# Forget logits from the value columns' sweep, key bias as rows for VectorE, reordered units of the mixer

## The chip, the core and the metric

The kernel runs on one core of a Trainium2 chip. The core has a matrix engine (TensorE, PE in the profile, with its weight loads as PEld), VectorE (DVE), ScalarE (ACT), GpSimd (POOL) and SyncE (SP), whose queue issues every DMA here. Each engine works through its own list in order and waits on semaphores for the others. SBUF is the memory on the core (128 partitions), PSUM takes the products of TensorE, DRAM is the memory outside. The metric is the device time of one launch in microseconds; lower is better.

## The reference

Two transformer blocks over 256 tokens of width 1024, in float32. The change lies in the mixer of the first block, whose input projection gives the queries, keys and values of a forgetting attention, its forget logits (eight columns), and four inputs of a gated recurrence:

```python
SPLITS = (FOX_WIDTH, FOX_WIDTH, FOX_WIDTH, FOX_HEADS, HGRN_WIDTH, HGRN_WIDTH, HGRN_WIDTH, HGRN_WIDTH)
hn = rmsnorm(h, norm_mix_g[l])
proj = hn @ w_in[l]
fq, fk, fv, ff, gq, gf, gi, gg = jnp.split(proj, split_idx, axis=-1)
log_f = jax.nn.log_sigmoid((ff + fox_f_bias[l]).astype(jnp.float32)).transpose(0, 2, 1)
fox_out = fox_attention(to_heads(fq), to_heads(fk), to_heads(fv), log_f)
...
F = jnp.cumsum(log_f, axis=-1)
s = jnp.einsum('bhqd,bhkd->bhqk', qi, k).astype(jnp.float32) * scale
s = s + Fi[..., None] - F[:, :, None, :]
s = jnp.where(mask, s, -jnp.inf)
p = jax.nn.softmax(s, axis=-1)
```

There are eight heads of width 64. The term of the query, F at t, is the same for a whole row of the softmax and falls out; the term of the key, minus F at s, is the key bias of the text.

## The kernel before

Every float32 product with a weight is made of three passes with operands split into a rounded high part and the rest: xh and xl for the activations, wh and wl for the weights. The weights stream in granules of 2048 values per partition (1 MB). SP loads a granule into one of three raw buffers, ScalarE casts half of it to wh (line 141), VectorE subtracts to get wl (line 142); six such halves, called parts, can stand ready.

The work is a list of units, one weight part each, with short pieces attached to them. A unit of a_units keeps weight blocks stationary and moves 256 token columns: 24 products. A unit of b_units keeps token blocks stationary and moves 512 weight columns: 12 products, six for token half t=0 and then six for t=1; four such units make 512 output columns and their sums are taken out of PSUM after the fourth. TensorE follows the list exactly as written. The other engines and SP get their order from a planner that works with the listed order as priority, so an operation of theirs can stand well before or after the place where it is listed.

The mixer has 36 units. Counted from 0: f (0 to 3) and q (4 to 7) of the recurrence, its gate (8 to 11), queries of the attention (12 to 15), its keys (16 to 19), its values (20 to 23), the recurrence's input gi (24 to 27), and keys of the memory for the cross attention (28 to 35). The pieces between them:

- The recurrence runs as nine levels, levels[0] to levels[8]: products on TensorE (lines 824, 804, 802, 853), then two decays (lines 813, 814) and a predicated copy on VectorE. The products of a level need the decays of the level before. They follow units 10, 11 and 13 to 19.
- forget() follows unit 12. It multiplies the eight logit columns of w_in, loaded on their own as wf (line 724) and split into wfh and wfl (lines 714, 715), in 24 products into one PSUM tile; then log-sigmoid and a cumulative sum on VectorE and ScalarE give minus F as high rows 0 to 7 and low rows 32 to 39 of the SBUF tile nF.
- For each of four pairs of heads there are three pieces: S (fox_scores, causal_exp), T (transposes of the probabilities) and V (products with the values). In S, two q k products of K = 64 per token tile are followed by two bias products (line 929): a selector column of sel, broadcast, times nF. The diagonal mask is added by VectorE in the pass that also finds the row's minimum (line 357); ScalarE takes the exponential; GpSimd and VectorE normalise each one half (line 938), one unit later. S of pairs 0 to 3 follows units 20, 21, 23 and 28; T 22, 25, 29 and 32; V 24, 27, 31 and 34.
- The memory rows are loaded after unit 12, normalised, and transposed after units 25 and 26 through PSUM tiles of the pool s, which has four buffers in turn. The differential attention's lambda is worked out by VectorE (line 737 and on) from small loads.

PSUM pools: mm and tp have two buffers each, s has four. The differential attention in block 2 has a piece of the same form as S, without bias products (line 1176).

## Time and profile before

| | |
|---|---|
| median of 3 runs | 922.87 us (921.74 to 923.49) |
| span of the profiled execution, first to last instruction | 918.8 us |
| TensorE busy | 904.6 us, 98% of the span |
| VectorE busy | 589.3 us, 64% |
| ScalarE busy | 489.4 us, 53% |
| GpSimd busy | 125.5 us, 14% |
| DMA | 160.79 MB, mean 175 GB/s |

The profiled execution's own time outside the span is not recorded; the 4.1 us between span and median stand for it. Times in the rows are microseconds from the span's start. Products are pipelined and their ends are modelled: what a product costs in a row of products is the step from its start to the next one's, not its duration. A bracket at the end of a timeline row says how long the engine was idle before it and which operation ended that.

### The profile page before, as it was taken

The page shows a single profiled execution, that of the slowest core. Times are in us where ns is not written, and L with a number is a line of the kernel's source. Part 1 is how long each engine was busy: PE and PEld are TensorE (multiplying, and loading weights), DVE is VectorE, ACT ScalarE, POOL GpSimd, SP SyncE. Part 2 cuts the span into 40 slices and gives each one's busy share as a digit, 9 for nine tenths or more (in the row PEclk, how much of TensorE's full clock was granted, in tenths as well). Part 3 has the DMA queues.
Part 4 walks back from the last instruction along what each step waited for, and adds up shares of the span by engine and source line. Part 5 has one row for each costly group of instructions (what it writes and reads, how often), then busy time and mean ns, then how long its engine had stood idle before and what let it go on. Part 6 is the DMA issues. An engine that isn't in the chain of part 4 may idle for free.

```text
span 918.8 us, 15164 instructions
## 1 busy us (share of the span) xinstructions
PE 904.6 (98%) x6203; PEld 823.5 (90%) x6203; DVE 589.3 (64%) x861; ACT 489.4 (53%) x741; POOL 125.5 (14%) x134
## 2 busy tenths in 40 slices
PE   8999999999999999999999999999999999999996
PEld 7889799899899999999899899999998789999995
DVE  5787666764675554445686555776656777766664
ACT  6763644555455444444564454657443676555552
POOL 3200110000002111111104000221301201101101
PEclk9999999999999999999999999999999999999998
DMA  8774344544465555565374555334655455555531
GB/s 260 253 245 141 130 153 169 197 148 138 161 204 184 185 184 183 184 186 188 134 271 139 184 181 187 128 115 140 216 178 190 159 185 182 186 199 192 167 131 46
DMA packets 116819, 160.79 MB, mean 175 GB/s; under 512 B 4551, under 2 KB 89357, under 8 KB 116749
## 3 DMA queue, kind: packets, MB, share of 16 engines
q1 hardware_dynamic: 116749, 159.82, 52.2%
q8 instruction: 48, 0.79, 0.3%
q14 instruction: 22, 0.18, 0.1%
HBM read 158.76 MB, written 1.05 MB: 174 GB/s over the span
## 4 chain that ended last, share of the span: by engine, by line
PE 89%; DVE 3%; DMA 2%; ACT 2%; issue 1%; POOL 1%; SPq 1%; DVEq 0%; POOLq 0%; ACTq 0%
PE mm L205 19%; PE mm L206 19%; PE mm L207 19%; PE s L206 8%; PE s L207 8%; PE s L205 8%; DMA w<-in_w_in_dram 2%; DVE wl L142 1%; PE s L804 1%; PE tp L336 1%; POOL sm L296 1%; PE tp L1032 1%; PE s L1024 1%; ACT wh L141 1%; DMA lamv<-in_lambda_k_dram 1%
## 5 line engine op out<-in xcount | busy, mean ns | idle before, releaser
L142 DVE TENSOR_TENSOR wl<-w,wh 128x1024 fp32r<-128x1024 f32 x283 | 354.0, 1257 | 191.8 <-ACT wh L141 190.1
L141 ACT CAST wh<-w 128x1024 fp32r<-128x1024 f32 x284 | 296.8, 1051 | 305.6 <-PE mm L206 199.2
L205 PE MATMUL mm<-xh,wh 128*128 128x256 f32 x1120 | 317.5, 283 | 0.4 <-ACT r L765 0.4
L206 PE MATMUL mm<-xl,wh 128*128 128x256 f32 x1120 | 313.1, 280 | 0.3
L207 PE MATMUL mm<-xh,wl 128*128 128x256 f32 x1120 | 312.5, 279 | 0.0
L205 PEld LDWEIGHTS mm<-xh,wh 128*128 128x128 f32 x1120 | 210.6, 188 | 4.3 <-issue 2.0
L206 PEld LDWEIGHTS mm<-xl,wh 128*128 128x128 f32 x1120 | 210.6, 188 | 2.1 <-DVE xl L328 0.7
L207 PEld LDWEIGHTS mm<-xh,wl 128*128 128x128 f32 x1120 | 210.5, 188 | 0.0
L205 PE MATMUL s<-wh,mh 128*128 128x512 f32 x176 | 70.1, 398 | 0.0
L206 PE MATMUL s<-wl,mh 128*128 128x512 f32 x176 | 69.6, 395 | 0.0
L207 PE MATMUL s<-wh,ml 128*128 128x512 f32 x168 | 66.4, 395 | 0.0
L296 POOL TENSOR_TENSOR sm<-sm,half 128x1 f32<-128x1 f32 (+2 forms) x24 | 20.2, 842 | 214.9 <-DVE sm L309 203.9
L1067 POOL TENSOR_TENSOR r<-r 128x512 f32<-128x512 f32 x16 | 25.4, 1584 | 149.1 <-ACT r L1065 149.1
L205 PE MATMUL mm<-eh,wh 128*128 128x256 f32 x160 | 45.6, 285 | 0.0
L206 PE MATMUL mm<-el,wh 128*128 128x256 f32 x160 | 44.7, 279 | 0.0
L207 PE MATMUL mm<-eh,wl 128*128 128x256 f32 x160 | 44.6, 279 | 0.0
L207 PE MATMUL s<-wh,mh 128*128 128x512 f32 x112 | 44.3, 396 | 0.0
L1326 POOL TENSOR_TENSOR r<-r 128x512 f32<-128x512 f32 x11 | 21.4, 1946 | 148.6 <-DVE r L1314 124.8
L206 PE MATMUL s<-wl,ml 128*128 128x512 f32 x104 | 41.1, 396 | 0.0
L205 PE MATMUL s<-wh,ml 128*128 128x512 f32 x104 | 41.1, 395 | 0.0
L205 PE MATMUL mm<-wh,xh 128*128 128x512 f32 x96 | 39.4, 410 | 0.5 <-ACT xh L324 0.4
L206 PEld LDWEIGHTS s<-wl,mh 128*128 128x128 f32 x176 | 33.1, 188 | 7.2
(272 smaller groups left out, 1365.3 us busy)
## 6 DMA issues: line engine op xcount, KB each, us to landing
w<-in_w_in_dram SPq DMA_DIRECT2D x41, 1024.0 KB, 5.3
w<-in_w_dram SPq DMA_DIRECT2D x32, 1024.0 KB, 4.8
w<-in_w_up_dram SPq DMA_DIRECT2D x22, 1024.0 KB, 5.0
w<-in_w_down_dram SPq DMA_DIRECT2D x11, 1024.0 KB, 5.1
w<-in_w_xkv_dram SPq DMA_DIRECT2D x8, 1024.0 KB
w<-in_w_out_dram SPq DMA_DIRECT2D x8, 1024.0 KB, 6.1
w<-in_w_xq_dram SPq DMA_DIRECT2D x4, 1024.0 KB, 4.7
w<-in_w_xo_dram SPq DMA_DIRECT2D x4, 1024.0 KB, 5.8
```

What stands on the lines that cost most here:

```text
L141: S.copy(hi, src)
L142: low.tensor_tensor(lo, src, hi.bitcast(F32), op=ALU.subtract)
L205: PE.matmul(o, lh, rh, start=first, stop=False)
L206: PE.matmul(o, lh, rl, start=False, stop=False)
L207: PE.matmul(o, ll, rh, start=False, stop=last)
L296: G.tensor_tensor(r[:, :n], v[:, :n], half.to_broadcast([P, n]), op=ALU.pow)
L336: PE.transpose(o[:, k * P:(k + 1) * P], xn[:, kk * P:(kk + 1) * P], ident)
L804: PE.matmul(o, k_[:, x], q2, start=True, stop=True)
L1024: PE.matmul(s[:, t, :], xq[:, j, t * P:(t + 1) * P], xkT[:, j, :], start=(c == 0), stop=(c == 1))
L1032: PE.matmul(o[:, c * T:(c + 1) * T], xv[:, m, cs], pt[:, m, :], start=(m == 0), stop=(m == 1))
L1067: G.tensor_tensor(tt, ra, ra, op=ALU.mult)
L1326: G.tensor_tensor(yv, yg, yv, op=ALU.mult)
```

## The change

The separate load, split and products of the eight logit columns go. The value columns are swept with 520 columns, values and logits together: fv_units makes two products of 260 columns where there was one of 512, in two mm and two tp tiles, and takes the logits out as two tiles of 128 tokens by eight, which forget() turns with two transposes. Minus F goes to a DRAM tile, negF, and comes back as rows on all partitions (load_bias, two DMAs a pair); GpSimd adds the diagonal mask to it; VectorE adds the result where it added the mask, so the bias products, nF and sel go. The values now stand in units 12 to 15, queries and keys alternate in 16 to 23. The levels follow units 9, 11, 12, 13, 14 and 16 to 19, forget() follows 15. S follows units 21, 23, 26 and 28; T 23, 27, 30 and 32; V 25, 29, 32 and 34. Comments are removed; nothing behind the mixer is touched.

```diff
     def causal_exp(s, bias):
...
-                V.tensor_tensor_reduce(pm[:, e, TILES[i]], s[e][:, TILES[i]], bias[:, (1 - i) * P:T], -1.0, 3e38,
+                V.tensor_tensor_reduce(pm[:, e, TILES[i]], s[e][:, TILES[i]], bias(e, i), -1.0, 3e38,
...
         def tables():
...
-            V.tensor_copy(r32(wfh), wf)
-            V.tensor_tensor(r32(wfl), wf, wfh, op=ALU.subtract)
-            V.tensor_tensor(r32(sel), ident[:, 0:8], ident[:, 32:40], op=ALU.add)
-            G.memset(nF, 0.0)
...
         def load_tables():
...
-                nc.sync.dma_start(wf.rearrange("p (k c) -> p k c", k=8),
-                                  w_in[:, 1536:1544].rearrange("(k p) c -> p k c", p=P))
...
+    def fv_units():
+        gs_ = [Granule(w_in[kq * 512:(kq + 1) * 512, 1024:1544], 4, 520, False) for kq in range(2)]
+        st = {}
+        def unit(i):
+            if i == 0:
+                st["o"] = [(mm_t(), tp_t()) for _ in range(2)]
+            w = part(gs_[i // 2], i % 2)
+            for t in range(2):
+                tok = slice(t * P, (t + 1) * P)
+                for k in range(2):
+                    for c in range(2):
+                        cs = slice(c * 260, (c + 1) * 260)
+                        mm3(st["o"][t][c][:, 0:260], r32(xh[:, 2 * i + k, tok]), r32(xl[:, 2 * i + k, tok]),
+                            w[0][:, k, cs], w[1][:, k, cs], i == 0 and k == 0, i == 3 and k == 1)
+            release()
+            def ev():
+                for t in range(2):
+                    copy = V.tensor_copy if t else S.copy
+                    o = st["o"][t]
+                    ff.append(sm_t())
+                    copy(fv[:, t, 0:260], o[0][:, 0:260])
+                    copy(ff[t], o[1][:, 252:260])
+                    copy(fv[:, t, 260:512], o[1][:, 0:252])
+            return ev if i == 3 else None
...
+    fox_bias = [x.rearrange("p (e c) -> p e c", e=2) for x in
+                (R[3][:, 1024:1792], R[0][:, 512:1280], R[0][:, 1280:2048], R[1][:, 0:768])]
     def forget():
-        o = tp_t()[0:8, 0:T]
-        wh, wl = (r32(x).rearrange("p (k c) -> p k c", k=8) for x in (wfh, wfl))
-        for k in range(8):
-            mm3(o, wh[:, k, :], wl[:, k, :], r32(xh[:, k, :]), r32(xl[:, k, :]), k == 0, k == 7)
-        z = R[3][0:8, 0:768].rearrange("p (i t) -> p i t", i=3)
+        o = s_t()[0:8, 0:T]
+        for t in range(2):
+            PE.transpose(o[:, t * P:(t + 1) * P], ff[t], ident)
+        z = p_t()[0:8, :].rearrange("p (i t) -> p i t", i=3)
...
-            V.tensor_copy(r32(nF[0:8, :]), z[:, 2, :])
-            V.tensor_tensor(r32(nF[32:40, :]), z[:, 2, :], nF[0:8, :], op=ALU.subtract)
-        then(cum)
+        then(cum, lambda: nc.sync.dma_start(negF, z[:, 2, :]))
+    def load_bias(*pairs):
+        def go():
+            for p in pairs:
+                row = negF[2 * p:2 * p + 2, :].rearrange("(o e) t -> o e t", o=1)
+                nc.sync.dma_start(fox_bias[p][:, :, 0:P], row[:, :, 0:P].to_broadcast([P, 2, P]))
+                nc.sync.dma_start(fox_bias[p][:, :, P:3 * P], row.to_broadcast([P, 2, T]))
+            def mask():
+                for p in pairs:
+                    for e in range(2):
+                        b = fox_bias[p][:, e, :].rearrange("p (n s) -> p n s", n=3)[:, 0:3:2, :]
+                        G.tensor_tensor(b, b, causal[:, P:T].unsqueeze(1).to_broadcast([P, 2, P]), op=ALU.add)
+            then(lambda: None, mask)
+        return go
     def fox_scores(p):
...
-                          start=True, stop=False)
-            for e in range(2):
-                hd = 2 * p + e
-                sh = r32(sel[:, hd:hd + 1]).to_broadcast([P, P])
-                PE.matmul(s[e][:, tile], sh, r32(nF[:, 0:(t + 1) * P]), start=False, stop=True)
-        pm, sums = causal_exp(s, causal)
+                          start=True, stop=True)
+        pm, sums = causal_exp(s, lambda e, i: fox_bias[p][:, e, TILES[i]])
...
+    u_ += fv_units()
+    for g in range(2):
+        u_ += a_units(cols(w_in, 0, g), XT, ev_to(R[2][:, g * 512:(g + 1) * 512], 0.125))
+        u_ += a_units(cols(w_in, 512, g), XT, ev_to(R[2][:, 1024 + g * 512:1024 + (g + 1) * 512]))
+    u_ += rows(w_in, 2568, 1, gi) + grid(xkw, 0, 4, R[5], None, ME)
     fox = Heads(fox_scores, fox_turn, fox_pv)
...
+    run(u_, {
+        1: [lambda: start.vectors()], 2: [lambda: start.load_tables()], 6: [lambda: start.tables()],
+        7: [lambda: start.load_later()], 9: [levels[0]], 11: [levels[1]],
+        12: [m_load, levels[2], lambda: start.difference()], 13: [levels[3]], 14: [levels[4]], 15: [forget],
+        16: [levels[5], m_s0], 17: [levels[6]], 18: [levels[7], m_s1, load_bias(0)], 19: [levels[8]],
+        20: [load_bias(1, 2, 3)], 21: [fox.S(0)], 23: [fox.T(0), fox.S(1)], 25: [fox.V(0), m_t0],
+        26: [fox.S(2), m_t1], 27: [fox.T(1)], 28: [fox.S(3), h_out(0)], 29: [fox.V(1), h_out(1)],
+        30: [fox.T(2)], 31: [h_turn(0)], 32: [fox.V(2), fox.T(3)], 33: [h_turn(1)], 34: [fox.V(3)],
+    })
```

## Rows read from the trace of the kernel before

**Rows 1.** Page part 1: busy time of each engine, share of the span, instructions; weight loads of part 5

```profile
PE 904.6 (98%) x6203; PEld 823.5 (90%) x6203; DVE 589.3 (64%) x861; ACT 489.4 (53%) x741; POOL 125.5 (14%) x134
L205 PEld LDWEIGHTS mm<-xh,wh 128*128 128x128 f32 x1120 | 210.6, 188 | 4.3 <-issue 2.0
```

**Rows 2.** Waits of TensorE, 20 to 220 us: who waited for whom, total us, times, longest

```profile
PE s L804 <- DVE r L825: 0.8, 1, 0.8
```

**Rows 3.** Windows table, 44.5 to 72 us: busy us and instructions of each engine, clock, DMA

```profile
44.50:72.00 27.50, 26.70 (x220) 25.19 (x219) 24.03 (x35) 16.61 (x25) 1.11 (x2) 1.00 0.74 253
```

**Rows 4.** Timeline of TensorE, 54 to 61 us: start, duration, line, operation, count

```profile
54.72 0.28 PE L205 MATMUL tp<-xh,wfh 128*8 128x256 f32 x1
...
57.45 0.28 PE L205 MATMUL mm<-xh,wh 128*128 128x256 f32 x1
...
60.25 1.89 PE L804 MATMUL s<-r,r 128*128 128x64 f32 x16
```

**Rows 5.** Timeline of TensorE, 90 to 101 us: first score piece and first transposes

```profile
91.04 0.49 PE L924 MATMUL s<-r 64*128 64x128 f32 x4
...
92.80 0.40 PE L205 MATMUL mm<-wh,xh 128*128 128x512 f32 x1
...
100.25 0.82 PE L345 MATMUL tp<-ident,P 128*128 128x128 f32 x6
```

**Rows 6.** Timeline of TensorE, 570 us: a score piece of block 2

```profile
570.06 0.93 PE L1176 MATMUL s<-r,r 64*128 64x128 f32 x8
570.91 0.38 PE L205 MATMUL mm<-xh,wh 128*128 128x256 f32 x1
```

**Rows 7.** Chain of waits, 90 to 101 us: start, us from step to step, operation

```profile
91.53 0.37 PE s L929 x2
...
99.95 0.23 PE mm L206
...
100.41 0.66 PE tp L345 x6
```

**Rows 8.** Timeline of TensorE at three unit ends: the first operation behind each

```profile
50.03 0.44 PE L804 MATMUL s<-r,r 128*128 128x64 f32 x2 [0.80 <-DVE r L825]
...
69.43 0.44 PE L804 MATMUL s<-r,r 128*128 128x64 f32 x3
...
78.60 0.44 PE L804 MATMUL s<-r,r 128*128 128x64 f32 x3
```

**Rows 9.** Timeline of VectorE near the same places

```profile
41.89 0.29 DVE L737 TENSOR_TENSOR lamv<-lamv 128x128 f32<-128x128 f32 x1 [3.65 <-DMA lamv<-in_lambda_k_dram]
...
70.04 2.34 DVE L142 TENSOR_TENSOR wl<-w,wh 128x1024 fp32r<-128x1024 f32 x2
...
78.80 0.69 DVE L269 COPY r<-mm 128x512 f32<-128x512 f32 x1 [0.57 <-PE mm L207]
```

**Rows 10.** Groups of VectorE, 0 to 160 us: busy us, mean ns, idle before

```profile
L325 DVE TENSOR_TENSOR ml<-tp,mh 128x256 fp32r<-128x256 f32 x4 | 1.7, 416 | 0.0
```

**Rows 11.** Timeline of VectorE: the forget scan and the first score operation

```profile
66.92 0.67 DVE L913 TENSOR_TENSOR_SCAN r<-r 8x256 f32<-8x256 f32 x1
...
93.36 0.28 DVE L357 CUSTOM_DVE_ANT_0 P<-s,causal 128x128 f32<-128x128 f32 x1
```

**Rows 12.** Timeline of GpSimd: two operations of one form, and the normalisation of pair 0

```profile
27.89 2.78 POOL L773 TENSOR_SCALAR r<-r 128x512 f32<-128x512 f32 x1 [11.77 <-DVE r L771]
...
31.45 1.06 POOL L773 TENSOR_SCALAR r<-r 128x512 f32<-128x512 f32 x1
...
95.93 0.84 POOL L938 TENSOR_SCALAR P<-P,sm 128x128 f32<-128x128 f32 x2 [35.81 <-DVE sm L934]
```

**Rows 13.** DMA issues of the whole span: queue, count, KB each, median us to landing

```profile
out_dram<-h SPq DMA_DIRECT2D x8, 128.0 KB, 1.8
...
g<-in_norm_mix_pre_dram SPq DMA_DIRECT2D x1, 512.0 KB, 6.9
```

**Rows 14.** Waits of the queue on SP, 0 to 240 us: total, times, longest

```profile
SPq L122 <- DVE wl L142: 130.1, 23, 9.0
```

More of the change, by code (lines that the diff above doesn't have):

```diff
@@ L60, in two_blocks @@
     small = ctx.enter_context(tc.tile_pool(name="small", bufs=16))
+    dram = ctx.enter_context(tc.tile_pool(name="dram", bufs=1, space=bass.MemoryType.DRAM))
     psum = ctx.enter_context(tc.tile_pool(name="psum", bufs=2, space=bass.MemoryType.PSUM))
@@ L611, in two_blocks @@
     lvl = const.tile([P, 512], U8, name="lvl")
-    sel = const.tile([P, 8], F32, name="sel")
-    nF = const.tile([P, T], F32, name="nF")
     vt = const.tile([P, 190], F32, name="vt")
@@ L620, in two_blocks @@
     pw = const.tile([P, 4, P], F32, name="pw")
-    wfh = const.tile([P, 64], F32, name="wfh")
-    wfl = const.tile([P, 64], F32, name="wfl")
+    negF = dram.tile([8, T], F32, name="negF")
     nlam = lam[:, 2:3]
@@ L683, in start @@
         lvlf = ppool.tile([P, 768], F32, tag="PT", name="lvlf")
-        wf = ppool.tile([P, 768], F32, tag="PT", name="wf")[:, 0:64]
         pieces = []
@@ L722, in load_tables @@
             nc.sync.dma_start(lvlf[:, 0:512], a["c_lvl"])
-            with nc.allow_non_contiguous_dma("eight columns"):
-                nc.sync.dma_start(wf.rearrange("p (k c) -> p k c", k=8),
-                                  w_in[:, 1536:1544].rearrange("(k p) c -> p k c", p=P))
             nc.sync.dma_start(fbias, a["fox_f_bias"].rearrange("o h -> h o"))
@@ L893, in h_turn @@
         return go
-    def forget():
-        o = tp_t()[0:8, 0:T]
-        wh, wl = (r32(x).rearrange("p (k c) -> p k c", k=8) for x in (wfh, wfl))
-        for k in range(8):
-            mm3(o, wh[:, k, :], wl[:, k, :], r32(xh[:, k, :]), r32(xl[:, k, :]), k == 0, k == 7)
-        z = R[3][0:8, 0:768].rearrange("p (i t) -> p i t", i=3)
+    ff = []
+    def fv_units():
[22 more added lines that the diff above has]
+            return ev if i == 3 else None
+        return [(lambda i=i: unit(i), gs_[i // 2] if i % 2 == 0 else None) for i in range(4)]
+    fox_bias = [x.rearrange("p (e c) -> p e c", e=2) for x in
+                (R[3][:, 1024:1792], R[0][:, 512:1280], R[0][:, 1280:2048], R[1][:, 0:768])]
+    def forget():
+        o = s_t()[0:8, 0:T]
+        for t in range(2):
+            PE.transpose(o[:, t * P:(t + 1) * P], ff[t], ident)
+        z = p_t()[0:8, :].rearrange("p (i t) -> p i t", i=3)
         V.tensor_scalar(z[:, 0, :], o, fbias, None, op0=ALU.add)
@@ L1177, in d_scores @@
                           start=True, stop=True)
-        pm, sums = causal_exp(s, bias)
+        pm, sums = causal_exp(s, lambda e, i: bias[:, (1 - i) * P:T])
         def norm():
```

10 lines of the change are left out of this document (removed).

## The prediction, made before the result was known

> **What bounds the kernel now.** I read the page first: TensorE is busy for 98% of the span, every other engine for 64% or less [rows 1]. Then the waits of TensorE in the mixer, which is the only stretch that the diff touches: from 20 to 220 us the list has two entries, and the larger is 0.8 us at the first level product behind VectorE's line 825 [rows 2]. So from 20 us on the kernel is a queue of products with no gap worth naming. Whatever leaves that queue leaves the time, and whatever makes TensorE wait adds to it. Last, the engine that could start to set the pace: in the stretch with the recurrence levels VectorE is busy 24.03 of 27.5 us, 87% [rows 3]. The weight loads are no bound: their queue entry mostly waits for VectorE to free a buffer [rows 14].
>
> **Removed: the forget products.** In the trace 24 products with an 8-column weight run from 54.72 to 57.45, when the next unit begins [rows 4]: 2.73 us of pure queue. Nothing else filled that time on TensorE. Minus 2.73 us.
>
> **Removed: the key bias products.** One score piece of the forgetting attention lasts from 91.04 to 92.80, 1.76 us [rows 5]; the other three pieces have the same pattern. Without the four bias products it is the piece that the differential attention of block 2 already has, same shapes and same K of 64: 570.06 to 570.91, 0.85 us [rows 6]. Four times 0.91 is 3.64 us. A lower bound is the smaller of a piece's two bias groups in the chain of waits, 0.37 us [rows 7], for each of the eight groups: 3.0 us. I take 3.64, since the block 2 piece is the same code without the bias.
>
> **Added: eight columns in the value sweep.** Four units go from 12 products of 512 columns (0.23 us each in the chain [rows 7], 2.8 us a unit) to 24 products of 260. The nearest unit has 24 products of 256 columns and takes 57.45 to 60.25, 2.80 us [rows 4]; times 260/256 is 2.84. Plus 0.04 a unit, with rounding plus 0.2 us for four. The price on the other side is the weight loads: 48 more, 188 ns each by the page [rows 1], 9.0 us if none were hidden. The 256-column unit has twice the loads of the 512-column one and the same length, so they are hidden, and I take 0.2.
>
> The Trainium skill speaks against this edit: TensorE: Matmul & The Clock Gate, Part 3 (The mechanism), says that a weight load overlaps products in flight only when their row groups differ, and all of these use every row. With the figure of the same page for a load (columns over 1.2, so 107 ns for 128 columns) 48 loads in the open would be an estimated 5.1 us, and the sum below would end at 922.2. The trace disagrees, by the two units of equal length.
>
> **Added: two transposes and their wait.** Six transposes take 0.66 us in the chain [rows 7], so two cost 0.2. The wait is new in kind: the transposes stand directly behind the last value product in TensorE's fixed order, and their input is the evicted 8-column piece. Half t=0 is complete half a unit earlier and ScalarE can take it out meanwhile; half t=1 goes through VectorE as a 260-column copy and then the 8-column one. An idle VectorE begins such a copy 0.2 us after the unit's end (78.60 and 78.80 [rows 8, 9]); 256 columns from PSUM take 0.42 us [rows 10], the small one less. So 0.4 (only the small copy is left) to 0.9 us if VectorE is idle. If it is behind, as at the unit end of 69.43, its splits run to 72.38 [rows 8, 9]: 2.9 plus 0.6, 3.5 us. The change leaves that unit's end without a level of its own, but the level before it is still being finished there. I take 1.0, near the idle end, and keep 0.4 to 3.5. Behind the waiting transposes stand all later products; nobody else waits for them soon.
>
> **Moved: the diagonal level goes from unit 10 to unit 9.** The 0.8 us wait at 50.03 is for VectorE's product of q and f [rows 2, 8]; one more unit (2.8 us) lies between the two now. Minus 0.8, with 0 as the other bound: VectorE had stood in line 737 until the lambda loads landed, at 41.89 [rows 9], and that wait may stay where it is. What is late next is the split of weights, which has buffers ahead.
>
> **Moved: the forget logits' way to the scores.** Before, the logits were a sum in SBUF 10.1 us after the last forget product (57.45, scan from 66.92 for 0.67 [rows 4, 11]). Now they also go to DRAM, come back as rows on all partitions, and GpSimd adds the mask. Write: 1.8 us, the landing time of the output rows; read: up to 6.9 us, the slowest broadcast of 512 KB (ours is 384 KB a pair) [rows 13]. Mask: two operations of 256 columns. The nearest GpSimd operation, 512 columns, took 1.06 us in one place and 2.78 beside VectorE's splits [rows 12], so half of that, 0.53 to 1.39 each. In sum, from the end of unit 15: 1.2 (wait and transposes), 10.1, 1.8, 6.9 and 1.1 to 2.8 is 21.1 to 22.8 us. The scores' VectorE operations of unit 21 need it after six units of 2.8, two level pieces of 1.9 (the row at 60.25 [rows 4]), leaving out two smaller ones, the 1.2, and 1.4 from the piece's start (2.3 before, 91.04 to 93.36 [rows 5, 11], less 0.9): 23.2. It fits by 0.4 us or more, so nothing on TensorE; if the cover is gone, each further microsecond arrives at the transposes of pair 0 after another 1.6 us. That spare: before, they began 9.2 us after the score piece (100.25 [rows 5]) and the normalisation ended 5.7 after it (95.93 plus 0.84 [rows 12]); now they come after 0.85 and two units, 6.45, against 4.8.
>
> The Trainium skill, SBUF — State Buffer (Who interferes with whom), says that a VectorE operation with two SBUF inputs and a GpSimd operation that reads SBUF shut each other out for a whole instruction. The 2.78 against 1.06 us agrees; by that rule the masks belong at the long end, which leaves the sum as it is and feeds the rivals below.
>
> **Other edits, at nothing.** The load of eight-column pieces, the two splits of it, the selector and one memset go from a stretch in which TensorE does not wait for them. Four more evictions of VectorE and ScalarE lie beside products. On SP's queue one write and eight loads stand among the weight loads; a weight load that comes late has the split buffers as cover, and the waits of that queue, up to 9.0 us [rows 14], cost TensorE nothing now. The second transpose of the memory rows has its PSUM tiles freed only one unit before, 0 to 1 us; I take 0.
>
> **Sum.** Minus 2.73, minus 3.64, plus 0.2, plus 0.2, plus 1.0, minus 0.8: minus 5.8 us. The span of the profiled execution is 918.8, the median of the three runs 922.87, so 4.1 us lie around the span and don't change. 922.87 less 5.8 is 917.1. With every unknown at its good end (wait 0.4, and another 0.4 us of the first waits gone) it is 916.1; with every one at its bad end (wait 3.5, the 0.8 kept, bias products at 3.0, 1 us at the memory rows) 922.0.
>
> **Rivals.**
> First, VectorE sets the pace between the levels: the 2.73 us of forget products were time in which it caught up, and it is 87% busy. Then the new wait is 3.5 instead of 1.0: 919.6. For it: the queue at 69.43. Against: at 78.60 it was idle at the same place.
> Second, the bias comes 1 to 4 us later than it may at the transposes of pair 0, through a slow load or masks: 918 to 921, middle 920. For it: the 0.4 us of cover. Against: each term of that chain was taken at its slow end.
> Third, slower. GpSimd works in order, and six masks of pairs 1 to 3 are listed ahead of the normalisation of pair 0. They wait for loads that may start only after unit 19, and if these stand behind a weight load for the 9.0 us seen on that queue, they land 15.9 us after unit 19; two masks after the last landing and the 0.84 make 19.5. The transposes are due after 12.1 (two units, 0.85, two units). TensorE then stands 7.4 us or, with all six masks after the landing, 12.9. The kernel is slower than before by more than can be taken for noise from a stall of 7.7 on; the middle is about 927. For it: the order of the list. Against: six masks before the scores' exponentials are done need no luck if the loads come soon.
> Fourth, the 48 extra weight loads come into the open: up to 9.0 us at 188 ns each, half of that 4.5, so 921.6 and no gain. For it: the load's length against the 0.12 us of a 260-column product. Against: the two units of equal length.
>
> **How the numbers follow.** My sum 0.62 (917.1, own range 915.5 to 919), the first rival 0.17 (919.6), the second 0.11 (920), the third 0.05 (927), the fourth 0.05 (921.6). A measurement of this kernel tells about 0.2%, 1.85 us, from no change: faster is below 921.0. Faster: 0.62, 0.17 and most of 0.11, so 0.86. Same: 0.05 and the rest, 0.08. Slower: 0.06. The range of 8 in 10 goes from 915.0 to 921.2; above it lie the third and the fourth case and a part of the second, below 916.1 only stalls that the trace does not show me.
>
> **What would show it.** The score piece lasts 0.85 us and no products with 8 columns are left. A value unit lasts 2.8 to 2.9; at 3.1 or more the weight loads came out. TensorE has one new entry in its waits, the forget transposes behind VectorE's copy, 0.4 to 3.5 us. The wait at the first level is gone. The transposes of pair 0 wait for nothing; if they do, GpSimd or a load is behind it and I am in the second or third case. The forecast is wrong if TensorE's idle time in the mixer grows by more than 3 us.

## The result and the profile after

The changed kernel takes 913.71 us (median of 4 runs, 913.16 to 916.50), the kernel before on the same chip 923.18 us (4 runs): ratio 0.9904, 95% interval 0.9887 to 0.9922. It is faster, by 9.5 us and not by the 5.8 of the forecast, and 913.71 lies below the range of 915.0 to 921.2. So the direction was right, and the size was wrong.

Four views of the changed kernel, in the order in which I read them. First, part 1 of the page: busy time of each engine, share of the span, instructions. TensorE has 6.6 us less to do than in [rows 1] and is as full as it was.

```profile
PE 898.0 (98%) x6213; PEld 823.9 (90%) x6213; DVE 588.4 (64%) x858; ACT 488.8 (54%) x743; POOL 130.0 (14%) x141
```

Second, the waits of TensorE from 20 to 220 us, the stretch of [rows 2] (who waited for whom: total us, times, longest). The wait at the first level is gone. The new entry at line 924 was foreseen, the larger one at line 346 was not.

```profile
PE tp L346 <- ACT PT L983: 0.6, 1, 0.6
PE s L924 <- DVE sm L910: 0.5, 1, 0.5
```

Third, the timeline of TensorE at the places of [rows 4, 5, 8] (start, duration, line, operation, count; the level pieces are clipped by the window asked for): the end of the gate sweep; a value unit; the forget transposes; the first score piece; the first transposes of probabilities; T(3); the start of the output stage.

```profile
48.46 0.78 PE L792 MATMUL s<-r,r 128*128 128x64 f32 x6
...
50.16 0.36 PE L206 MATMUL mm<-wh,xh 128*128 128x260 f32 x1
...
53.13 1.11 PE L792 MATMUL s<-r,r 128*128 128x64 f32 x9
...
67.14 0.27 PE L924 MATMUL s<-ident,sm 128*8 128x128 f32 x1
67.90 0.27 PE L924 MATMUL s<-ident,sm 128*8 128x128 f32 x1 [0.49 <-DVE sm L910]
67.93 0.37 PE L206 MATMUL mm<-xh,wh 128*128 128x256 f32 x1
...
90.79 0.93 PE L961 MATMUL s<-r 64*128 64x128 f32 x8
91.65 0.39 PE L206 MATMUL mm<-xh,wh 128*128 128x256 f32 x1
...
97.46 0.82 PE L346 MATMUL tp<-ident,P 128*128 128x128 f32 x6
...
136.05 0.55 PE L346 MATMUL tp<-ident,P 128*128 128x128 f32 x3
137.17 0.55 PE L346 MATMUL tp<-ident,P 128*128 128x128 f32 x3 [0.57 <-ACT PT L983]
137.47 0.36 PE L206 MATMUL mm<-eh,wh 128*128 128x256 f32 x1
...
147.81 0.40 PE L206 MATMUL s<-wh,mh 128*128 128x512 f32 x1
```

The score piece lasts from 90.79 to 91.65, 0.86 us. The value unit lasts 2.97. To see where the two profiled executions part, here are four lines: the first product of the gate sweep and of the output stage in before, then the first product of the gate sweep and the last product of all in the changed kernel.

```profile
35.70 0.39 PE L205 MATMUL mm<-wh,xh 128*128 128x512 f32 x1
...
153.39 0.39 PE L205 MATMUL s<-wh,mh 128*128 128x512 f32 x1
```

```profile
35.19 0.40 PE L206 MATMUL mm<-wh,xh 128*128 128x512 f32 x1
...
905.28 0.40 PE L208 MATMUL s<-wh,ml 128*128 128x512 f32 x1
```

The output stage begins 5.58 us earlier. Of these, 0.51 lie ahead of the gate sweep and 5.07 between it and the output stage, where all terms of the sum have their place; 5.8 were foretold. The surplus lies elsewhere.

Fourth, GpSimd's timeline, for the way of the logits: masks of pair 0, masks of the other pairs, normalisation of pair 0.

```profile
84.02 3.16 POOL L951 TENSOR_TENSOR r<-r,causal 128x256 f32<-128x256 f32 x2 [8.16 <-DMA r<-negF]
90.62 2.57 POOL L951 TENSOR_TENSOR r<-r,causal 128x256 f32<-128x256 f32 x4 [3.45 <-DMA r<-negF]
93.63 1.81 POOL L951 TENSOR_TENSOR r<-r,causal 128x256 f32<-128x256 f32 x2 [0.44 <-issue]
95.82 0.90 POOL L971 TENSOR_SCALAR P<-P,sm 128x128 f32<-128x128 f32 x2 [0.38 <-DVE sm L967]
```

One correction to the forecast's ground stands in the runs themselves: the changed kernel's profiled execution took 914.16 us with a span of 912.3, and every other profiled execution also has 1.8 us around its span. So the profiled execution of before, span 918.8, took about 920.6 and not 922.87: it was an execution 2.3 us better than the median, and the waits in it were small ones. The shortest of the 108 executions of this kernel timed in later comparisons took 920.72, so the profile shows the best case.

### The profile page after: what moved, and what is told of

The parts are those of the page before. It is cut to its first block, busy times and chain, and to the rows that moved or that the text cites. A ratio compares the mean times of both kernels' runs of the same rounds, so it can differ in the third digit from the quotient of the medians.

```text
span 912.3 us, 15217 instructions
## 1 busy us (share of the span) xinstructions
PE 898.0 (98%) x6213; PEld 823.9 (90%) x6213; DVE 588.4 (64%) x858; ACT 488.8 (54%) x743; POOL 130.0 (14%) x141
## 4 chain that ended last, share of the span: by engine, by line
PE 90%; DVE 4%; ACT 2%; DMA 2%; POOL 1%; issue 1%; SPq 0%; DVEq 0%; POOLq 0%; ACTq 0%
PE mm L206 19%; PE mm L207 19%; PE mm L208 19%; PE s L208 8%; PE s L206 8%; PE s L207 8%; DMA w<-in_w_in_dram 2%; PE s L792 1%; POOL sm L297 1%; DVE wl L143 1%; PE tp L1068 1%; PE s L1060 1%; PE tp L337 1%; ACT wh L142 1%; PE s L1212 1%
## 5 line engine op out<-in xcount | busy, mean ns | idle before, releaser
L143 DVE TENSOR_TENSOR wl<-w,wh 128x1024 fp32r<-128x1024 f32 (+1 forms) x283 | 355.4, 1261 | 182.4 <-ACT wh L142 180.8
L142 ACT CAST wh<-w 128x1024 fp32r<-128x1024 f32 (+1 forms) x284 | 296.1, 1048 | 306.0 <-PE mm L207 190.2
L206 PEld LDWEIGHTS s<-wh,mh 128*128 128x128 f32 x176 | 33.1, 188 | 6.7
```

The lines of the kernel that those rows point to most:

```text
L142: S.copy(hi, src)
L143: low.tensor_tensor(lo, src, hi.bitcast(F32), op=ALU.subtract)
L206: PE.matmul(o, lh, rh, start=first, stop=False)
```

## The experiments

**Both kernels again, and the diagonal level alone.** `b_again` is the kernel before and `a_again` the changed kernel, without any edit. `b_lev9` and `a_lev10` exchange the place of the diagonal level:

```diff
 b_lev9 (from before)
-             7: [lambda: start.load_later()], 10: [levels[0]], 11: [levels[1]]})
+             7: [lambda: start.load_later()], 9: [levels[0]], 11: [levels[1]]})
 a_lev10 (from the changed kernel)
-        7: [lambda: start.load_later()], 9: [levels[0]], 11: [levels[1]],
+        7: [lambda: start.load_later()], 10: [levels[0]], 11: [levels[1]],
```

> The kernel before once more, unchanged, timed against itself. It tells whether the profiled execution (span 918.8 us, so about 920.6 with the 1.8 us that lie around the span of every execution of the kernel after) is typical of the timed ones (921.7 to 923.9). Theory A, a cliff at the start: in most executions the wait at the first level product (0.8 us in the profile) is longer, because the lambda loads that VectorE stands waiting for land later; then the new profile shows more than 0.8 there, up to 3.5, and its span grows by the same. Theory B, the pace of the products: the span differs by some tenths of a per cent through all stages alike, with the same waits. Ratio 1.000 in both.

> The kernel before with one part of the change alone: the diagonal level follows unit 9 instead of 10. Theory A: the wait at the first level product goes whole, 3 to 4 us in the timed runs, ratio about 0.996. Theory B: only the 0.8 to 1.0 us of the profile go, ratio 0.999.

> The kernel after with that part undone: the diagonal level follows unit 10 again, everything else as in the change. Theory A: 3 to 4 us of the 9.5 come back, about 917, ratio to the kernel before 0.994. Theory B: 0.8 to 1.0 come back, ratio 0.991 to 0.992.

> The kernel after once more, unchanged, on the same chip as the three others. The first comparison gave a ratio of 0.9904 (0.9887 to 0.9922), my sum 0.9937. Theory A: 0.990 again. Theory B, chance differences of pace between single executions: nearer to my sum, 0.992 to 0.994.

Measured: b_again 923.43 (ratio to before 0.9983 to 1.0016), b_lev9 920.77 (0.9969 to 0.9991), a_lev10 914.57 (0.9889 to 0.9928), a_again 915.45 (0.9891 to 0.9931). The earlier level is worth 0.8 to 2.9 us in before and nothing in the changed kernel, whose waits have no entry at the first level in either place. So neither theory holds whole. a_again, with 0.9911, lies nearer to A's 0.990 than to B's 0.992 to 0.994 and doesn't exclude them. The waits of TensorE in b_again, 20 to 220 us, show why one profile was a bad ground:

```profile
PE mm L205 <- ACT r L765: 1.7, 1, 1.7
PE s L804 <- DVE r L825: 0.4, 1, 0.4
```

The same program had 0.4 and 0.8 in the first profile (the 0.8 is [rows 2], the 0.4 the other entry of that view); when TensorE is held up ahead of the level, it waits less at the level. In the nine other profiles of kernels with before's order of levels (b_again, b_wf, b_pad, b_pad32, the three b_sh, b_spl96, b_cut) the wait at the first level was 0.4 to 1.9 us. The alignment of a_again with b_again showed something else that nobody had listed: the 512-column products ran 1% faster in all profiles of the changed kernel (mean step to the next product 232.4 ns in a_again, 235.0 in b_again). What reaches all products is the place of the weight buffers: they became wider (1040 instead of 1024 values a part), and constants ahead of them went (sel, 32 bytes, among them).

**Placement, the start's load, and the bias by itself.** Four kernels: before with the wide buffers, nF put into ml to make room, and nothing else (`b_pad`); the changed kernel with the bias products back (`a_bias`); the changed kernel with the eight-column load back at its old place (`a_wf`); before with that load moved out of the start (`b_wf`).

```diff
 b_pad (from before)
-            g.raw = wraw.tile([P, g.nk, g.ncol], F32, tag="w", name=nm("w"))
+            raw = wraw.tile([P, 2080], F32, tag="w", name=nm("w"))
+            g.raw = raw[:, 0:2048].rearrange("p (k c) -> p k c", k=g.nk)
...
-        hi = wspl.tile(shape, F32R, tag="wh", name=nm("wh"))
+        hi = wspl.tile([P, 1040], F32R, tag="wh", name=nm("wh"))
...
-    nF = const.tile([P, T], F32, name="nF")
+    nF = ml[:, 7, :]
 a_bias (from the changed kernel)
...
-                          start=True, stop=True)
-        pm, sums = causal_exp(s, lambda e, i: fox_bias[p][:, e, TILES[i]])
+                          start=True, stop=False)
+            for e in range(2):
+                hd = 2 * p + e
+                sh = r32(sel[:, hd:hd + 1]).to_broadcast([P, P])
+                PE.matmul(s[e][:, tile], sh, r32(nF[:, 0:(t + 1) * P]), start=False, stop=True)
+        pm, sums = causal_exp(s, lambda e, i: causal[:, (1 - i) * P:T])
...
 a_wf (from the changed kernel)
...
+                nc.sync.dma_start(wf.rearrange("p (k c) -> p k c", k=8),
+                                  w_in[:, 1536:1544].rearrange("(k p) c -> p k c", p=P))
```

> The kernel before with one thing of the change alone that computes nothing: each weight buffer is as wide as the change makes it (1040 instead of 1024 values for a split part, 2080 instead of 2048 for a load), so that every later buffer lies at another address; the 1-KB tile nF lies in a part of ml that is not yet in use, to make room. The 512-column products were about 1% faster in all three profiles with the wide buffers than in both with the narrow ones. Theory C (the pace of these products hangs on where the operands lie): the mean of a 512-column product falls from 395 to 391-394 ns, the stretches behind the mixer that take 174.77, 45.95 and 69.53 us before take about 174.2, 45.7 and 69.3, and the time falls by 1.5 us (about 921.8 against 923.3). Theory D (the pace comes from the other edits, or from when buffers are written): the stretches stay at 174.77, 45.95 and 69.53 and the time within 0.3 us of before's.

> The changed kernel with the key bias back as products of TensorE (sel and nF as before, nF in a part of ml that is not yet in use; no DRAM row, no row loads, no masks on GpSimd). It prices the second part alone. The prediction's own step: 4 score pieces of 1.76 us instead of 0.86, so +3.6 us (about 918.0 where the changed kernel has 914.4). Rival E (the row loads and the masks slow something that the prediction put at nothing, and this part's net gain is smaller): +2 to +3. Rival F (the score pieces' products hide a wait of VectorE or ScalarE that comes out elsewhere): pieces of 1.76 but an end less than 2 us later, since a later wait such as the 0.6 us one at T(3) goes.

> The changed kernel with the load of the eight forget columns back at its old place on SP ahead of two weight loads in the start; nothing reads it. Theory G (this load of 32-byte pieces held up the second weight load, so that ScalarE's conversion and with it TensorE's wait at line 205 came later; the prediction put its going at nothing): the conversion that starts at 22.9-23.1 us in the two profiles of the changed kernel starts at 23.6-24.9, TensorE waits 0.4-1.7 us at line 205 for ScalarE's result of the head unit, and the time is 1.3 to 2.5 us above the changed kernel's (about 916.5). Rival H (those starts scatter by chance): within 0.4 us of the changed kernel.

> The kernel before with the load of the eight forget columns (and the two instructions that split it) moved behind the start: the load goes out with the later tables at unit 7, the split at unit 10. Theory G (the load in the start costs 1.3 to 2.5 us): about 921.4, and the conversion starts near 23.0 us instead of 23.6-24.9, the wait at line 205 gone or below 0.4. Rival H (chance): 923.3, as before. A wait at the forget products would show that the load came too late at its new place.

Measured: b_pad 931.35 (ratio 1.0061 to 1.0100), a_bias 927.29 (1.0027 to 1.0061), a_wf 914.69 (0.9882 to 0.9922), b_wf 922.00 (0.9976 to 1.0004). The load in the start is worth nothing that can be measured, in either kernel: rival H. But the two kernels that were meant to differ by 1.5 and 3.6 us from before and the changed kernel came out at 931.35 instead of 921.8 and at 927.29 instead of 918.0, against every theory on record. Both have the padded buffers and nF inside ml. No wait accounts for it: the loss grows evenly over all products to the end of the program. From the first product of the output stage on, b_pad falls behind b_again by 1.5 us after 1100 products, 4.4 after 3100 and 7.5 after 5100. The program's memory map names the suspect: split weights start at 96 modulo 128 bytes in before, at 64 and 0 in turn in the changed kernel, and at 96 and 32 in turn in these two.

**Nothing but placement.** `a_sh32`, `b_sh32` and `b_sh96` widen one constant (g8, the last one) by 32, 32 and 96 bytes; `b_pad32` is b_pad with sel inside ml as well, which takes 32 bytes away.

```diff
 a_sh32, b_sh32 (32; b_sh96 has 32 where these have 16, b_sh64 has 24)
-        g = const.tile([P, 8], F32, name="g8")
+        g = const.tile([P, 16], F32, name="g8")[:, 0:8]
 b_pad32 (from b_pad)
-    sel = const.tile([P, 8], F32, name="sel")
+    sel = ml[:, 6, 0:8]
```

> The changed kernel with one tile of the constants 32 bytes wider, so that every later buffer lies 32 bytes higher; nothing else is different. The split weight buffers then start at 96 and 32 modulo 128 in turn, as in the two runs that came out long (b_pad, a_bias), instead of 64 and 0. Theory C (the pace of all products hangs on this start): 256-column products at 283 instead of 280 ns and 512-column products at 396 instead of 392, so about 923.7, 9 us above the changed kernel, and a_bias (927.3) stands 3.6 above it. Theory D (the loss of those two came from the tile nF that was laid into ml): 914.4, as the changed kernel.

> b_pad again (the kernel before with weight buffers as wide as the change makes them, nF in ml), with sel in ml too, so that all later buffers lie 32 bytes lower and the split weight buffers start at 64 and 0 modulo 128 in turn, exactly as in the changed kernel. Theory C: the products go back to 280 and 392 ns and the time from 931.4 to about 922; what then stands between this and the changed kernel (914.4) is the work of the change alone, 7 to 8 us. Theory D (nF in ml): 931.4 again.

> The kernel before with one tile of the constants 32 bytes wider: the weight buffers keep their width, and all start at 0 modulo 128 instead of 96. Theory C: the 512-column products come down from 395 to about 392 ns, as with the buffers at 64 and 0; the 256-column products keep 280 or come down too, where units of 24 of them take 2.74 us in some buffers of the changed kernel against 2.80 in before. That is 1.5 us if only the former gain, up to 10 us if all units take 2.74: 913 to 921.8. Theory D (placement does nothing): 923.3.

> The kernel before with the weight buffers at 64 modulo 128 (one tile of the constants 96 bytes wider, all else as before). Theory C with a rule by 64 bytes: the same as b_sh32 (buffers at 0). With a rule by 128 bytes it differs from it. Theory D: 923.3.

Measured: a_sh32 924.40, b_pad32 921.71, b_sh32 928.84, b_sh96 916.22 us, where before took 922.64. The first two were foretold at 923.7 and 922: theory C, and nF in ml costs nothing. b_sh32 came out above both forecasts (913 to 921.8 and 923.3), since all buffers at 0 turned out worse than at 96. The changed kernel, moved by 32 bytes, is no faster than before (ratio 1.0001 to 1.0030). Before, moved by 96 bytes and with no other edit, has two thirds of the change's gain (0.9905 to 0.9946).

The trace shows it in the stretch that is the same program in all: from the first product of the output stage to the last one. Timeline of TensorE, b_again, then b_sh96, then a_again, then a_sh32:

```profile
155.89 0.39 PE L205 MATMUL s<-wh,mh 128*128 128x512 f32 x1
...
913.92 0.40 PE L207 MATMUL s<-wh,ml 128*128 128x512 f32 x1
```

```profile
155.56 0.40 PE L205 MATMUL s<-wh,mh 128*128 128x512 f32 x1
...
907.59 0.40 PE L207 MATMUL s<-wh,ml 128*128 128x512 f32 x1
```

```profile
147.81 0.40 PE L206 MATMUL s<-wh,mh 128*128 128x512 f32 x1
...
904.19 0.40 PE L208 MATMUL s<-wh,ml 128*128 128x512 f32 x1
```

```profile
152.46 0.40 PE L206 MATMUL s<-wh,mh 128*128 128x512 f32 x1
...
917.97 0.40 PE L208 MATMUL s<-wh,ml 128*128 128x512 f32 x1
```

758.03, 752.03, 756.38 and 765.51 us. Before and the changed kernel differ by 1.65 us here, where they compute the same with the same instructions; b_pad32, which is before at the changed kernel's placement, takes 756.42 and so agrees with the changed kernel to 0.04. Six profiles of before's placement lie between 757.99 and 758.05, three of the changed kernel's between 756.25 and 756.38. The first profile of the changed kernel is the exception, with 757.47: it has one wait in this stretch that the others lack:

```profile
PE s L1134 <- ACT r L272: 0.8, 1, 0.8
```

By the medians the move from before's placement to the changed kernel's is worth 0.9 us in before (b_pad32, ratio 0.9981 to 1.0002), which alone is not clear of noise; the traces carry that claim, the times of b_sh96 and a_sh32 the larger one that placement counts.

At equal placement the change is worth 921.71 less 914.6 (the mean of 913.71, 914.57 and 915.45), 7.1 us, and by the other pair 931.35 less 924.40, 7.0 us. These medians come from different chips; by the ratios to before in each comparison the two pairs give 7.7 and 6.0. The bias products alone, a_bias less a_sh32, are 2.9 us by the medians, also from two chips: rival E's range of 2 to 3, and not the 3.6 of the prediction. In the traces of these two, from the forget transposes to T(3), they are 3.2 (72.83 and 69.61 us).

**What the left-out products are worth, which buffers count, and a better version.** `b_cut` is before without 21 of the 24 forget products and without the bias products; `b_spl96` puts the 96 bytes between the loads and the split weights; `a_all64` sets the split buffers of the changed kernel 4224 bytes apart instead of 4160, so that all start at 64 modulo 128; `a_best` also moves T(3).

```diff
 b_cut (from before)
-        for k in range(8):
-            mm3(o, wh[:, k, :], wl[:, k, :], r32(xh[:, k, :]), r32(xl[:, k, :]), k == 0, k == 7)
+        mm3(o, wh[:, 0, :], wl[:, 0, :], r32(xh[:, 0, :]), r32(xl[:, 0, :]), True, True)
...
-                PE.matmul(s[e][:, tile], sh, r32(nF[:, 0:(t + 1) * P]), start=False, stop=True)
 a_all64 (from the changed kernel)
-        hi = wspl.tile(shape, F32R, tag="wh", name=nm("wh"))
+        hi = wspl.tile([P, 1056], F32R, tag="wh", name=nm("wh"))
...
-    lamv = const.tile([P, 4, 64], F32, name="lamv")
+    lamv = R[2][:, 0:256].rearrange("p (a b) -> p a b", a=4)
 a_best (from a_all64)
-        30: [fox.T(2)], 31: [h_turn(0)], 32: [fox.V(2), fox.T(3)], 33: [h_turn(1)], 34: [fox.V(3)],
+        30: [fox.T(2)], 31: [fox.T(3)], 32: [fox.V(2)], 33: [h_turn(0)], 34: [fox.V(3)], 35: [h_turn(1)],
```

> The kernel before with 21 of the 24 forget products and all eight bias products of each of the four score pieces left out: the forget logits come from one of eight blocks and the key bias is missing, all else as before, buffers included. The prediction's own prices: forget 2.73 us, of which 3 of 24 products stay (-2.4), bias 4 x 0.91 (-3.64), together -6.0: about 916.9 against 922.9. Rival J (products that run between waits hide something): less than 5. Rival K (these products cost more than their own time, by what they delay): more than 7.

> The kernel before with a gap of 96 bytes between the buffers of the weight loads and those of the split weights: the loads stay where they were, the split buffers start at 64 modulo 128 as in b_sh96. If it is TensorE's reading of the split buffers that hangs on their start, this gives b_sh96's time, 916.2, and its stretches (512-column products 393 ns). If it is where the loads land, it gives before's, 922.9, or something between.

> The changed kernel with split weight buffers 4224 instead of 4160 bytes apart, so that all, not every other one, start at 64 modulo 128 (lamv lies in a part of R[2] that is not yet in use, to make room). From the last 5200 steps of TensorE: 762.1 us with all at 64, 766.7 with 64 and 0 in turn. So 4.6 us faster than the changed kernel: about 910, if the start modulo 128 is all that counts. If the distance of the buffers counts too (4096 in b_sh96, 4224 here), anything between 910 and 919.

> a_all64 with T(3) one unit ahead of V(2) instead of behind it in the same piece, and the two h_turn pieces one and two units later, so that the copy of T(3)'s first half has a unit's products beside it. The wait of TensorE for the copy at T(3) (0.6 us, gap 0.81) goes: 0.6 to 0.8 us below a_all64, if nothing comes late behind; a wait at h_turn(1) or at V(3) would show that the gain went there.

Measured: b_cut 917.52 against 922.57, 5.1 us (ratio 0.9911 to 0.9959, 3.8 to 8.2 us): the forecast's 6.0 lies inside, rivals J and K are not excluded by the time. b_spl96 915.41: b_sh96's time with the loads unmoved (and 752.30 us in the stretch), so it is the place of the split buffers, or of what lies behind them, and not where the loads land. a_all64 906.64, ratio 0.9789 to 0.9838: 8 us below the changed kernel where 4.6 were expected, and below the 910 to 919 left open, so something beside the start counts, the distance of the buffers or what moves with it. a_best 906.63: no difference in time. In its trace the end of the sweep to the output stage takes 0.8 us less and the wait at T(3) is gone, but unit 0 began 2 us later: in the start TensorE waited 1.97 us for VectorE at line 670 instead of 0.86, and worked at half clock behind it. The windows view of a_best (busy us and instructions of TensorE, its weight loads, VectorE, ScalarE, GpSimd; then the granted clock, DMA):

```profile
12.00:16.00 4.00, 3.33 (x15) 3.21 (x16) 3.17 (x8) 3.22 (x9) 0.57 (x2) 0.50 0.91 284
```

Nine of the twenty profiles have a mean clock of 0.50 to 0.67 there, three of the eight of the changed kernel and its variants and six of the twelve of before and its variants; in before and in a_all64 it is 1.00. The stretch of a_all64:

```profile
147.50 0.39 PE L207 MATMUL s<-wh,mh 128*128 128x512 f32 x1
...
896.43 0.40 PE L209 MATMUL s<-wh,ml 128*128 128x512 f32 x1
```

748.93 us. The groups of TensorE by form (busy us, mean ns of one) show that the 256-column products themselves are shorter, as far as modelled ends can; b_again first, a_all64 second:

```profile
L207 PE MATMUL mm<-xh,wl 128*128 128x256 f32 x1120 | 313.2, 280 | 0.0
...
L207 PE MATMUL s<-wh,ml 128*128 128x512 f32 x168 | 66.4, 395 | 0.0
```

```profile
L209 PE MATMUL mm<-xh,wl 128*128 128x256 f32 x1120 | 310.7, 277 | 0.0
```

The mean step from a 256-column product to the next one, 120.7 ns in b_again and 118.5 in a_all64, says the same.

**The level wait, and the fourth start.** b_cut's trace had shown what a long wait at the first level brings. The windows of b_cut around a wait of 1.7 us at line 804:

```profile
50.00:54.00 4.00, 3.02 (x17) 3.03 (x18) 1.56 (x2) 1.99 (x5) 0.00 (x0) 0.72 0.99 373
54.00:58.00 4.00, 4.00 (x20) 4.00 (x21) 3.67 (x5) 0.44 (x2) 0.23 (x1) 0.50 0.85 329
```

TensorE stood, then worked without a gap at half clock (1.2 of 2.4 GHz). b_pad32 (wait 1.9) shows the same at 0.92 and 0.66. Waits of 0.8 us and less at this level had no such stretch behind them, and b_spl96's of 1.5 had none either. b_again has its stretch elsewhere, behind the 1.7 us at line 205:

```profile
32.00:36.00 4.00, 4.00 (x24) 4.00 (x24) 3.96 (x6) 3.97 (x6) 1.83 (x3) 0.63 0.83 263
```

`b_lat` takes the wait out of before by order; `b_sh64` is the last start.

```diff
 b_lat (from before)
-             7: [lambda: start.load_later()], 10: [levels[0]], 11: [levels[1]]})
+             7: [lambda: start.load_later()], 10: [levels[0]]})
-        0: [forget, m_load], 1: [levels[2], lambda: start.difference()], 2: [levels[3]], 3: [levels[4]],
+        0: [levels[1], forget, m_load], 1: [levels[2], lambda: start.difference()], 2: [levels[3]], 3: [levels[4]],
```

> The kernel before with levels[1] one unit later, after the first unit of the query grid instead of the last one of the gate sweep, so that VectorE's product of line 825 has a whole unit more; all else as before, buffers included. Theory L (the first level's wait costs before its own 0.3 to 1.9 us and, in the executions in which it is long, a stretch at half clock on top): the wait at line 804 is gone, the granted clock stays at 1.00 from 50 us on, and the time falls by 1.0 to 2.5 us, to 920.2-921.7 against 922.7. Theory M (the wait only moves to the next level, or to the forget products behind it): 922.7.

> The kernel before with all weight buffers at 32 modulo 128 (one tile of the constants 64 bytes wider). The starts 96, 0 and 64 took 768.2, 772.6 and 762.1 us for the last 5200 steps of TensorE, and 96 and 32 in turn 775.9. If every buffer's pace hangs on its own start, 32 is the slowest: 783 us for those steps, and 937 in all. If it hangs on the pair of neighbouring buffers too, between 768 and 783.

Measured: b_lat 922.12 against 923.59 (ratio 0.9972 to 0.9999, 0.1 to 2.6 us), the wait gone and the clock full at this place:

```profile
50.00:54.00 4.00, 4.00 (x27) 3.60 (x26) 2.66 (x4) 2.13 (x3) 0.00 (x0) 1.00 1.00 343
54.00:58.00 4.00, 4.00 (x38) 3.65 (x37) 2.56 (x5) 3.69 (x10) 0.55 (x1) 1.00 1.05 409
```

Theory L fits, and theory M's zero lies just outside the interval. From 54 us on a 256-column product follows the last one after 0.12 us here and after 0.21 in b_cut. b_sh64 took 928.94, and 763.28 in the stretch: 32 is bad, but not the worst, and 96 and 32 in turn (765.5) are worse than either alone, so "each buffer by its own start" falls.

## Why the prediction was right, and where it was wrong

All placements beside each other. The stretch is that from the output stage's first product to the last product.

| split weights start at (mod 128), distance | kernels | stretch, us | median, us |
|---|---|---|---|
| 96, 4096 | before (b_again) | 758.0 | 922.6 to 923.6 |
| 32, 4096 | b_sh64 | 763.3 | 928.9 |
| 0, 4096 | b_sh32 | 762.2 | 928.8 |
| 64, 4096 | b_sh96, b_spl96 | 752.0, 752.3 | 916.2, 915.4 |
| 96 and 32, 4160 | b_pad; a_sh32 | 765.6; 765.5 | 931.4; 924.4 |
| 64 and 0, 4160 | b_pad32; changed (a_again) | 756.4; 756.4 | 921.7; 913.7 to 915.5 |
| 64, 4224 | a_all64 | 748.9 | 906.6 |

**Wrong: "Other edits, at nothing".** The width of the value sweep's tiles was counted as 0.04 us a unit of products. It also widened every weight buffer, and the going of sel took 32 bytes away ahead of them; both moved the buffers. That is 1.65 us behind the mixer in the traces of a_again and b_again, in a stretch that I never looked at since the diff doesn't touch it. It was luck in size and sign: the width without sel's 32 bytes is b_pad, 8.7 us slower than before, and with 32 bytes more the change is no gain (a_sh32).

**Wrong, and the larger part of the miss: "so 4.1 us lie around the span and don't change".** 1.8 do. The sum was made against an execution of 920.6 us and then taken from a median of 922.87. The other 2.3 us are the distance of this execution from the median, time that a usual execution of before spends somewhere inside the span, and in the first comparison it went with the change. Between the two profiled executions the change is worth 6.45 us, near the 5.8 of the sum; between the medians 9.47. With that, minus 0.8 for the level wait was the size of one good execution. The term was right in sign and place, and mis-sized: the wait goes up to 1.9 us and can bring half clock with it, and b_lat and b_lev9 price it, by medians, at 1.5 and 2.5 us. That the earlier level is what removes it isn't so either: a_lev10 has the old place and no wait. A lighter start seems to do it as well, but a_wf puts the load back with the level early, so the pair isn't complete, and which edit frees VectorE in a_lev10 is open.

**Right: the mixer of one execution against one.** 5.07 us from the gate sweep to the output stage, where the sum said 5.8; the nearness has some luck in it, since misses of both signs, listed here, offset each other. By its steps:
- Forget products, minus 2.73: gone from the timeline. Together with the bias products they are worth 5.1 us in b_cut, where 6.0 were foretold; its interval, 3.8 to 8.2, holds both. No run prices them alone.
- Bias products, minus 3.64: score pieces of 0.86 us as foretold from [rows 6]; a_bias against a_sh32 says 3.2 by the trace, since products beside the shorter pieces take a little more (5.83 against 5.74 us, 5.81 against 5.71). The lower bound of 3.0 was as near.
- Value units, plus 0.2: 2.97 us each instead of 2.84, so at most 0.5. The weight loads did not come out: 48 of them in the open would have been units of 5 us. The Trainium skill (TensorE: Matmul & The Clock Gate, Part 3, The mechanism) has a weight load overlap products in flight only when their row groups differ; that again is not what this trace shows for these products.
- Forget transposes and their wait, 1.2: 67.14 to 67.93, 0.79, with 0.49 of wait. VectorE was idle enough, the first rival fell. In the window of [rows 3] it is now busy for 21.30 us.
- Not foreseen: T(3) stands directly behind V(2) in one piece, and its second half waits for ScalarE's copy: 1.42 us instead of 0.57 (both from a_all64 and a_best). The diff says so in plain text, "32: [fox.V(2), fox.T(3)]"; I read the forget and bias edits and passed over what the new order puts next to what.

**Right, with other spares than said: the way of the logits.** From the end of the sweep, 67.14, to the end of pair 0's masks, 84.02 plus 3.16, it took 20.0 us where 21.1 to 22.8 were foretold. VectorE's first score operation stands at 91.86, 1.07 us after the score piece began, so the bias was ready 4.7 us ahead of its use, not 0.4. (The profile puts VectorE's wait there down to the loads of negF; in a_lev10, with the same 1.64 us of wait, it names the scores of line 961.) Write and read were shorter, the masks longer: 1.58 us each, past the long end of 1.39, beside VectorE's splits, and 0.64 each in the row at 90.62, where VectorE was busy for half of the time. That is the direction of the rule cited in the forecast (the Trainium skill, SBUF — State Buffer, Who interferes with whom): a VectorE operation with two SBUF inputs contends with a GpSimd operation that reads SBUF. The masks of pairs 1 to 3 end at 95.44, the normalisation behind them at 96.72, and the transposes begin at 97.46: a wait there was 0.7 us away where the forecast had 1.65 to spare. The masks did not set that: they ended 0.38 us before the normalisation began, which waited for VectorE (the bracket in its row). For the third rival's slower kernel the stall would have had to reach 7.7 us, so its 0.05 was not shown to be too low.

Put together, for the two profiled executions, 6.45 us of span: 0.51 ahead of the gate sweep, 5.07 in the mixer behind it, 0.55 in the stretch behind the mixer (1.65 without the wait at line 1134), 0.3 behind the last product (not looked into). The medians are 3.0 further apart, since the profiled execution of before was 2.6 us better than its median there (923.18) and the changed kernel's 0.45 worse. Later comparisons have 7.9 us between the medians (a_again) and 8.7 (a_lev10), so the 9.5 of the first one is itself at the long end.

That those 3.0 are waits and half clock is shown in part. Of the 108 executions of before, the 25 with a mean granted clock of 0.993 or less took 924.0 to 926.8 us, the 26 with 0.997 or more 920.7 to 924.1. None of the 24 of b_lev9 and b_lat and none of the 20 of the changed kernel, a_lev10 and a_wf lies below 0.994. So the slowest executions are missing where the wait at the first level is gone. How much the waits at line 205 and in the start add, and why the eight profiles of the changed kernel and its variants have none at line 205, stays open.

## What to carry to other kernels

When an edit changes the size of any tile, the kernel after is another placement: compare both kernels at equal placement, by a shift of 32 to 96 bytes in a constant, before the difference is put down to the edit, and look for the best placement as a change of its own (here 906.64 us, 16 us below before instead of 8 to 9.5). A wait in one profile is one draw: take three profiles of the kernel before, and read the granted clock behind each wait. Check the time of the profiled execution itself, not its span against a median.

## What was not expected of the hardware

TensorE's float32r products go up to 2.2% slower or faster (765.5 against 748.9 us for the same products) with nothing changed there but where the split weights, and the small buffers behind them, lie. At a distance of 4096 bytes 64 modulo 128 was the best of the four starts (752.0), and 0 and 32 cost 4.2 and 5.3 us against 96 in the stretch; at 4224 only 64 was tried. The Trainium skill, SBUF — State Buffer (Operand start alignment), asks of an operand that it starts at a multiple of its element size, and says that this is about legality and not speed. Every kernel here keeps that, and the pace differs. Why it does, whether reads of TensorE or writes of ScalarE and VectorE into the same buffers are slowed, and why 4224 bytes of distance are better than 4096, no run here tells.

A wait of 1.3 to 1.9 us at the first level was followed by some 4 us in which the mean granted clock was 0.50 to 0.66 in four kernels (b_cut, b_pad, b_pad32, b_sh96) and by none in a fifth (b_spl96, 1.52 us); waits of 0.3 to 0.8 us there were not followed by any. At line 205 a wait of 1.75 us in b_again was followed by such a stretch, and one of 1.25 in b_sh96 by none. So the price of a wait can have a step in it, and which waits meet it isn't told by their length alone.
